# Summed weights first, a fourth staging slot, and the last feature tile held back, in a two-layer encoder trunk

## Chip, core and metric

The kernel runs on one core of a Trainium2 chip. TensorE (PE) multiplies, VectorE (DVE) and ScalarE (ACT) work element by element, GpSimd (POOL) issues some transfers and fills a few tiles, and SyncE (SP) issues most transfers. The metric is the device time of one execution in microseconds (us).

## What is computed

Two requests of 256 rows each run through the same two-layer encoder with shared weights. In front of each stand 16 meta rows, which are dropped at the end. Each layer adds a mixer (retention and grouped attention) and then a SwiGLU of width 2816 to the residual; the width of the model is 1024.

```python
def _mixer(h, w_in, ...):
    proj = h @ w_in
    rq, rk, rv, rg, aq, ak, av, gr, ga = jnp.split(proj, split_idx, axis=-1)
    ...
    merged = jax.nn.sigmoid(gr) * ret + jax.nn.sigmoid(ga) * att
    return merged @ w_out

def _swiglu(h, w_ffn_in, w_ffn_out):
    a, u = jnp.split(h @ w_ffn_in, 2, axis=-1)
    return (jax.nn.silu(a) * u) @ w_ffn_out

def _trunk(x, ...):
    h = jnp.concatenate([meta_tokens, x], axis=1)          # 16 + 256 rows
    ...
    for l in range(DEPTH):                                 # 2 layers
        h = h + _mixer(_rms(h, norm_mix[l]), w_in[l], ...)
        h = h + _swiglu(_rms(h, norm_ffn[l]), w_ffn_in[l], w_ffn_out[l])
    return _rms(h, norm_final)[:, N_META:]
```

## The kernel before

**Products.** All products keep fp32 accuracy: each operand is split into a rounded high part and the rest (`wh`, `wl` for weights, `xh`, `xl` for activations), and each tile product is three matmuls, high by high, high by low, low by high. The high part is a cast on ACT, the low part a subtraction on DVE (L214 and L215 for plain weights, L238 and L242 for the staged ones). In layer 0 a request has 272 columns, in layer 1, where the meta rows are no longer needed, 256; layer 1 takes both requests in one matmul of 512 columns where it can.

**The first matrix of the SwiGLU.** Its 22 feature tiles are done in three groups, 0 to 7, 8 to 14 and 15 to 21. The first three tiles of a layer are plain (`fa`, `fu`). The other 19 per layer are done by a seven-product scheme of the Strassen kind, `product(f, i)` for i from 0 to 6, each product four k-steps of three matmuls, twelve matmuls of 272 or 256 columns. It mixes the two requests (`T0`, `T1`, `T2` are sums of their activations) and the weights: per feature tile f there are the summed weights c (tile `wc`: the up-weights, to which two accumulating DMAs on POOL's queue, L225 and L226, add another half of the up-weights and half of the gate-weights), a (tile `wa`, the gate-weights as they are), b (tile `wb`, made on DVE from `wa` and `wc` at L250 and L251) and d (tile `wst`). Products 0 and 4 use a, 1 and 5 use b, 2 and 3 use c, 6 uses d. In the trace all of them are `sp`, or `p` for 5 and 6.

**Staging.** `wc` and `wa` of all f, and before the first f of a layer the mixed activations `xn`, share the tag `q` of three slots. A slot can be loaded again when its last reader on DVE has run: for `wc` that is the low part of c (`cl`, L242), for `wa` the low part of a (`wl`, L242). The high and low part of c have one buffer each, `ch` and `cl`.

**Order.** `plan` gives each load and each step of the splitting (`s_load`, `s_1` to `s_4`) a due time, a lead in units of four products ahead of the f that needs it. A scheduler then fixes the order of each engine's instructions; at run time every engine, and SP's and POOL's queues, go strictly in that order, so an instruction that waits holds up all behind it.

**The end of a feature tile.** After products 2 and 3, L882 to L884 combine their PSUM banks with product 1; L884 is the last reader of the bank of product 2. Products 0 to 4 take turns in a `lin` and an `att` bank. After product 6, DVE L891, tanh on ACT L892, DVE L893 and L894, a cast on ACT (`oh`, L304) and DVE L305 (`ol`) make the tile's output.

**The second matrix.** After each group, `out` runs eight output tiles j for each request (`fo`), each accumulating over all feature tiles of the group, seven or eight times three matmuls. It begins with j = 0 and 1, for both requests, and the last feature tile of the group is the last that a `fo` unit needs. In the residual `f`, L915 then adds the unit. The attention of layer 1 begins behind the last group of layer 0, with the table `rel` (L449) and the decays `dm` (L708, L709) made from it; `rope` and nine zeroed tiles (`v80`, `p80`, `pm80`) stand in a pool that is never closed.

Of the kernel before, what the change touches and what calls it, by code (L numbers as in the profile page):

```python
# [90 lines left out]
def hybrid_kernel(tc, ctx, a, y_dram):  # L91
# [13 lines left out]
    def f32(t):  # L105
        return t.bitcast(F32)
# [30 lines left out]
    def tab(i, s, c0, q=slice(None)):  # L137
        if s == BOTH:
            t = rope[q, i, M:].unsqueeze(1)
            return t.to_broadcast([t.shape[0], 2, S])  # L140
        return rope[q, i, c0:]

# [8 lines left out]
    open_tmp(0)  # L151
    cst = const.tile([P, NCST + 44], F32, name="cst")
    rope = const.tile([P, 4, N], F32, name="rope")

# [11 lines left out]
    dec = cst[:, ng + 2 * DEPTH:NCST]  # L166
    v80s = [const.tile([80, P], F32R, name=f"v80_{i}") for i in range(5)]
    p80s = [const.tile([80, N], F32R, name=f"p80_{i}") for i in range(2)]
    pm80s = [const.tile([80, 64], F32R, name=f"pm80_{i}") for i in range(2)]
    for t in v80s + p80s + pm80s:  # L170
        G.memset(f32(t), 0.0)
    turn = {"v": 0, "p": 0, "m": 0}

    def nxt(kind, ring):
        turn[kind] += 1
        return ring[(turn[kind] - 1) % len(ring)]

# [52 lines left out]

    def s_tmp(name, tag="q", bufs=3):
        return E["wk"].tile([P, KT, P], F32, tag=tag, name=name, bufs=bufs)

    def s_hi(w, nm):
        pool, tg, n, bufs = {"a": (wts, "w", KT, NW), "b": (wts, "w", KT, NW),
                             "c": (E["wk"], "c", KT, 1), "d": (E["wk"], "d", NK, 1)}[nm]
        w[nm] += [pool.tile([P, n, P], F32R, tag=tg + x, name=tg + x, bufs=bufs) for x in "hl"]
        A.copy(w[nm][1], w[nm][0])  # L238
# [6 lines left out]
    def s_1(key):  # L245
        w = wready[key[1:3]]
        s_hi(w, "a")
        va, vb, vc = w["a"][0], s_tmp("wb", "wb", 1), w["c"][0]
        w["b"] = [vb]
        V.tensor_tensor(vb[:, :NK], va[:, :NK], vc[:, NK:], ALU.add)  # L250
        V.scalar_tensor_tensor(vb[:, NK:], va[:, NK:], -1.0, vb[:, :NK], ALU.mult, ALU.subtract)  # L251

    def s_2(key):
        w = wready[key[1:3]]
        s_hi(w, "b")
        s_lo(w, "a")
# [37 lines left out]

    def mm(ps, key, hi, lo, s, c0):
# [123 lines left out]
    def L(key, s, post):  # L419
        prog.append((key, s, post))  # L420
# [4 lines left out]
    def layer(l):  # L425
# [11 lines left out]
        def open_att():  # L437
            E["nqk"], E["nqk2"], E["nv"] = NWK[l]
            if not first:
                E["c1"].close()  # L440
                open_tmp(l)
            E["xh"], E["xl"] = grid(tx + "h", F32R), grid(tx + "l", F32R)
            E["sg"] = grid("f", F32)
            E["cm"], E["c1"] = ExitStack(), ExitStack()
            mpp = E["cm"].enter_context(tc.tile_pool(name=f"mp{l}", bufs=1))
            E["mp"] = grid("mp", F32, pool=mpp)
            E["wk"] = E["c1"].enter_context(tc.tile_pool(name=f"wka{l}", bufs=1))
            E["rel"] = E["wk"].tile([P, 2, DW], F16, name="rel")
            nc.sync.dma_start(E["rel"], a["rel"])  # L449

# [51 lines left out]
        def val2(key):  # L502
            vt = st.pop(("vt", key))
            pt = att("vps")
            for c, w, i in KCH:
                T.transpose(pt[:, i * P:(i + 1) * P], vt[:, c:c + w], ident)
            v = E["wk"].tile([P, 2, 2, P], F32R, tag="v", name="v", bufs=E["nv"])
            split(v[:, 0], v[:, 1], pt[:, :2 * P].rearrange("p (c d) -> p c d", c=2))
            if first and key[2]:
                v80 = st.pop(("v80", key[:2]))  # L510
            else:
                T.transpose(pt[:M, 2 * P:3 * P], vt[:, :M], ident)
                v80 = nxt("v", v80s)
# [108 lines left out]
        def att_t(s, hq):  # L622
            ps = st.pop(("p", s, hq))
            pt = E["wk"].tile([P, 2, 2, N - q0], F32R, tag="pt", name="pt", bufs=2)
            p80 = nxt("p", p80s)
            tp = att("ptp")
# [31 lines left out]
        def meta_t(s, g):  # L658
# [6 lines left out]
            split(ptm[:, 0], ptm[:, 1], tp[:, :P].rearrange("p (c d) -> p c d", c=2))  # L665
            p80 = nxt("m", pm80s)
            A.copy(p80[0:16], tp[:M, 128:192])
# [45 lines left out]
        def ret_s(s, hr):  # L713
            q, k, dm = st.pop(("rq", s)), st.pop(("rk", s)), st["dm", hr]
            pt = E["wk"].tile([P, 2, 2, N - q0], F32R, tag="pt", name="rpt", bufs=2)
            p80 = nxt("p", p80s)
            for c, w, i in KCH:
# [97 lines left out]
        def norm_x(s, k):  # L815
            if s and k % NK == 0:
                E["xn", k // NK] = E["wk"].tile([P, NK, N - q0], F32, tag="q", name="xn", bufs=3)
            for i in (k, k + 1):
# [36 lines left out]

        def product(f, i):
            w = wready[l, f]
# [16 lines left out]
            t1, u2 = st["tu"][:, 0], st["tu"][:, 1]  # L874
            if i == 1:
                V.tensor_tensor(u2, ps, t1, ALU.subtract)
            elif i == 2:
                st["p5"] = ps
            elif i == 3:
                st["yw"], st["c"], p5 = two("yw"), two("c", 4), st.pop("p5")  # L880
                y, v = st["yw"][:, 0], st["yw"][:, 1]
                V.tensor_tensor(v, ps, u2, ALU.add)  # L882
                V.tensor_tensor(y, p5, u2, ALU.add)
                V.scalar_tensor_tensor(st["c"][:, 3], v, -1.0, p5, ALU.mult, ALU.subtract)  # L884
            elif i == 4:
                V.tensor_tensor(st["c"][:, 0], ps, t1, ALU.add)
                st["v"] = two("v")
# [48 lines left out]

        def U(kind, j, s, rhs, c0, post, *args, bank=lin):
            L((l, kind, j), s, (rhs, c0, post, args, bank))

# [125 lines left out]
        for gi, (f0, f1) in enumerate(GROUPS):  # L1065
# [44 lines left out]
    prefetch(-1)  # L1110
    nc.sync.dma_start(rope, a["rope"])
    for k in range(0, KT, 4):
        nc.sync.dma_start(E["h"][1][:, k:k + 4], a["x"][1, :, k:k + 4])
    for key, f, rest in prog:
        if key is None:
            f(*rest)
            continue
        prefetch(pos[key])
        if key[0] == "sp":
            rest[0](*rest[1:])  # L1120
            slot[0] += 0.5
        else:
            rhs, c0, post, args, bank = rest
            hi, lo = rhs()
            ps = bank(key[1])
            mm(ps, key, hi, lo, f, c0)
            slot[0] += 2 if f == BOTH else 1
            post(ps, *args)
        due(slot[0])
# [40 lines left out]
```

## Time and profile before

| | us |
|---|---|
| median of three runs | 1891.21 (1889.67 to 1892.96) |
| the profiled execution | 1892.1 |
| its span | 1890.3 |
| PE busy | 1812.6 |
| DVE busy | 1293.2 |
| ACT busy | 862.6 |

The profiled execution lies 0.9 us over the median. Times in rows are counted from the start of the span. The three groups of layer 0 run from about 590 to 930, those of layer 1 from about 1510 to 1835. A releaser in brackets is the instruction or transfer on which the idle engine waited last. The granted clock of PE is a share of 2.4 GHz; it has two levels, 2.4 and 1.2 GHz, and a window shows a mean.

### The profile page before, as it was taken

How to read it: one execution, taken by the hardware profiler on the slowest of the kernel's cores; microseconds unless marked ns; L12 is line 12 of the kernel's file. 1: busy time of each engine (PE TensorE's matmuls, PEld its weight loads, DVE VectorE, ACT ScalarE, POOL GpSimd, SP SyncE). 2: the span in 40 equal slices, each digit the busy share in tenths (PEclk: the TensorE clock that was granted, in tenths of full speed). 3: DMA queues.
4: the chain of work that ended last, by engine and by line, in shares of the span. 5: the costliest groups of instructions: out<-in, count | busy, mean ns of one | idle time of the engine just before them, and what ended most of it. 6: DMA issues, size and time to landing. Idle time of an engine off the chain costs nothing.

```text
span 1890.3 us, 33475 instructions
## 1 busy us (share of the span) xinstructions
PE 1812.6 (96%) x13002; PEld 1712.7 (91%) x13002; DVE 1293.2 (68%) x2948; ACT 862.6 (46%) x1833; POOL 76.5 (4%) x107
## 2 busy tenths in 40 slices
PE   9999999999999899799899999999999998988997
PEld 8999999999999899799898888889888987987996
DVE  7777777775468747647787677667744886575685
ACT  7777753443334424323456666434433443332443
POOL 0000000000001101001000000000000010010100
PEclk9999999999999999899999999999999999999999
DMA  4222122224225635535242221122243365364442
GB/s 149 90 71 76 60 65 68 79 79 133 90 84 134 184 84 135 138 83 147 80 133 90 68 79 57 67 90 68 69 143 101 98 158 152 93 152 124 113 126 70
DMA packets 95104, 192.73 MB, mean 102 GB/s; under 512 B 10336, under 2 KB 18784, under 8 KB 94944
## 3 DMA queue, kind: packets, MB, share of 16 engines
q1 hardware_dynamic: 81136, 163.15, 27.2%
q0 software_dynamic: 12576, 26.35, 7.6%
q8 instruction: 102, 1.67, 0.4%
q10 hardware_dynamic: 1232, 1.08, 0.2%
q14 instruction: 58, 0.48, 0.1%
HBM read 186.35 MB, written 4.19 MB: 101 GB/s over the span
## 4 chain that ended last, share of the span: by engine, by line
PE 69%; DVE 12%; DMA 11%; ACT 4%; issue 4%; DVEq 0%; POOL 0%; ACTq 0%; POOLq 0%
DMA wc<-in_w_ffn_in 6%; PE fo L299 4%; PE fo L300 4%; PE fo L301 4%; DMA wst<-in_w_ffn_out 2%; DMA wa<-in_w_ffn_in 2%; PE rv L300 2%; PE rv L299 2%; PE rv L301 2%; PE ao L300 2%; PE ao L301 2%; PE ao L299 2%; PE aq L299 2%; PE gr L301 2%; PE gr L300 2%
## 5 line engine op out<-in xcount | busy, mean ns | idle before, releaser
L214 ACT CAST wh<-wst 128x512 fp32r<-128x512 f32 (+1 forms) x424 | 250.9, 610 | 367.6 <-PE fo L300 73.9
L215 DVE TENSOR_TENSOR wl<-wst,wh 128x512 fp32r<-128x512 f32 (+1 forms) x424 | 281.7, 677 | 126.6 <-ACT wh L214 120.5
L299 PE MATMUL fo<-oh,wh 128*128 128x272 f32 (+2 forms) x616 | 190.5, 310 | 25.6 <-ACT oh L304 25.6
L300 PE MATMUL fo<-ol,wh 128*128 128x272 f32 (+2 forms) x616 | 189.9, 309 | 0.0
L301 PE MATMUL fo<-oh,wl 128*128 128x272 f32 (+2 forms) x616 | 189.2, 308 | 0.0
L299 PEld LDWEIGHTS fo<-oh,wh 128*128 128x128 f32 x616 | 119.1, 194 | 31.5 <-ACT oh L304 27.5
L300 PEld LDWEIGHTS fo<-ol,wh 128*128 128x128 f32 x616 | 119.5, 194 | 5.4 <-DVE ol L305 1.3
L301 PEld LDWEIGHTS fo<-oh,wl 128*128 128x128 f32 x616 | 119.7, 194 | 4.1
L915 DVE SCALAR_TENSOR_TENSOR f<-fo,f 128x272 f32<-128x272 f32 (+2 forms) x84 | 39.5, 471 | 110.1 <-PE fo L301 109.7
L869 PE MATMUL sp<-xh,wl 128*128 128x272 f32 (+1 forms) x304 | 87.3, 287 | 2.3 <-DVE wl L242 2.3
L867 PE MATMUL sp<-xh,wh 128*128 128x272 f32 (+1 forms) x304 | 87.4, 287 | 0.0
L868 PE MATMUL sp<-xl,wh 128*128 128x272 f32 (+1 forms) x304 | 86.9, 286 | 0.0
L238 ACT CAST wh<-wa 128x1024 fp32r<-128x1024 f32 x38 | 39.8, 1048 | 86.9 <-PE fo L300 52.4
L250 DVE TENSOR_TENSOR wb<-wa,wc 128x512 f32<-128x512 f32 x38 | 26.3, 692 | 75.3 <-DMA wc<-in_w_ffn_in 57.4
L299 PE MATMUL wo<-mh,wh 128*128 128x272 f32 (+2 forms) x224 | 67.8, 303 | 0.0
L300 PE MATMUL wo<-ml,wh 128*128 128x272 f32 (+2 forms) x224 | 67.4, 301 | 0.0
L301 PE MATMUL wo<-mh,wl 128*128 128x272 f32 (+2 forms) x224 | 67.4, 301 | 0.0
L867 PE MATMUL sp<-xh,ch 128*128 128x272 f32 (+1 forms) x152 | 46.6, 307 | 19.1 <-DVE c L884 19.0
L225 POOL DMA_DIRECT2D wc<-in_w_ffn_in x38 | 32.7, 862 | 786.4 <-DMA wc<-in_w_ffn_in 198.1
L869 PEld LDWEIGHTS sp<-xh,wl 128*128 128x128 f32 x304 | 58.0, 191 | 2.5 <-DVE wl L242 2.5
L238 ACT CAST wh<-wb 128x1024 fp32r<-128x1024 f32 x38 | 39.6, 1043 | 42.3 <-DVE wb L251 28.8
L867 PEld LDWEIGHTS sp<-xh,wh 128*128 128x128 f32 x304 | 58.2, 191 | 0.0
(428 smaller groups left out, 6412.4 us busy)
## 6 DMA issues: line engine op xcount, KB each, us to landing
wst<-in_w_in SPq DMA_DIRECT2D x208, 256.0 KB, 2.7
wc<-in_w_ffn_in SPq DMA_DIRECT2D x38, 512.0 KB, 3.6
wc<-in_w_ffn_in POOLq DMA_DIRECT2D x76, 256.0 KB, 5.8
wa<-in_w_ffn_in SPq DMA_DIRECT2D x38, 512.0 KB, 4.6
wst<-in_w_ffn_out SPq DMA_DIRECT2D x64, 256.0 KB, 3.0
wst<-in_w_ffn_in SPq DMA_DIRECT2D x62, 256.0 KB, 3.0
wst<-in_w_att_o SPq DMA_DIRECT2D x32, 256.0 KB, 2.8
wst<-in_w_ret_o SPq DMA_DIRECT2D x32, 256.0 KB, 2.8
```

The costliest lines, as they stand in the source:

```text
L214: A.copy(wh[:, k:k + n], st[:, :n])
L215: V.tensor_tensor(wl[:, k:k + n], st[:, :n], f32(wh)[:, k:k + n], ALU.subtract)
L225: nc.gpsimd.dma_start(c[:, NK:], fu[:, :NK], accum_op=ALU.add)
L238: A.copy(w[nm][1], w[nm][0])
L250: V.tensor_tensor(vb[:, :NK], va[:, :NK], vc[:, NK:], ALU.add)
L299: T.matmul(out, wh[:, k], at(hi, s, k, c0), start=(k == 0), stop=False)
L300: T.matmul(out, wh[:, k], at(lo, s, k, c0), start=False, stop=False)
L301: T.matmul(out, wl[:, k], at(hi, s, k, c0), start=False, stop=(k == kt - 1))
L867: T.matmul(ps, wh[:, o], xh[:, k], start=k == 0, stop=False)
L868: T.matmul(ps, wh[:, o], xl[:, k], start=False, stop=False)
L869: T.matmul(ps, wl[:, o], xh[:, k], start=False, stop=k == NK - 1)
L915: V.scalar_tensor_tensor(hh, of(ps, s, q0), 0.5, hh, ALU.mult, ALU.add)
```

## The change

It has three parts, and line numbers of the new kernel are 4 to 8 higher.

1. For every f but the first of a layer's 19, products run in the order 2, 3, 0, 1, 4, 5, 6: the two with the summed weights come first. The splitting goes with it: `wb` and the high part of c in `s_1`, low part of c and high of a in `s_2`, and so on, each lead a quarter larger. The combinations of L882 to L886 come after product 1, which is now the fourth.
2. The tag `q` has four slots and the pair for d two. The room comes from `rope` and the nine zeroed tiles, which move to the attention's pool and are thus loaded and zeroed once for each layer. In layer 0 SP loads `rope` behind the second request's rows; in layer 1 the nine memsets, `rope` (557 KB) and `rel` stand on POOL's queue, the memsets behind the last product of layer 0, and before the `hd` transfers (L929).
3. `out` does j = 0 and 1 in two parts: first all feature tiles but the last for every one of these units, then the last tile for every one. The fourth unit of layer 0 takes an `att` bank. This holds for `wo` too.

```diff
@@ hybrid_kernel: tables and rings
-            t = rope[q, i, M:].unsqueeze(1)
+            t = E["rope"][q, i, M:].unsqueeze(1)
...
-    cst = const.tile([P, NCST + 44], F32, name="cst")
-    rope = const.tile([P, 4, N], F32, name="rope")
+    cst = const.tile([P, NCST + 76], F32, name="cst")
...
-    v80s = [const.tile([80, P], F32R, name=f"v80_{i}") for i in range(5)]
-    p80s = [const.tile([80, N], F32R, name=f"p80_{i}") for i in range(2)]
-    pm80s = [const.tile([80, 64], F32R, name=f"pm80_{i}") for i in range(2)]
-    for t in v80s + p80s + pm80s:
-        G.memset(f32(t), 0.0)
+    def open_rings():
+        wk = E["wk"]
+        E["rope"] = wk.tile([P, 4, N], F32, name="rope")
+        E["v"] = [wk.tile([80, P], F32R, name=f"v80_{i}") for i in range(5)]
+        E["p"] = [wk.tile([80, N], F32R, name=f"p80_{i}") for i in range(2)]
+        E["m"] = [wk.tile([80, 64], F32R, name=f"pm80_{i}") for i in range(2)]
+        for t in E["v"] + E["p"] + E["m"]:
+            G.memset(f32(t), 0.0)
@@ staging slots and split steps
-    def s_tmp(name, tag="q", bufs=3):
+    def s_tmp(name, tag="q", bufs=4):
...
-                             "c": (E["wk"], "c", KT, 1), "d": (E["wk"], "d", NK, 1)}[nm]
+                             "c": (E["wk"], "c", KT, 1), "d": (E["wk"], "d", NK, 2)}[nm]
...
-        s_hi(w, "a")
         va, vb, vc = w["a"][0], s_tmp("wb", "wb", 1), w["c"][0]
         w["b"] = [vb]
         V.tensor_tensor(vb[:, :NK], va[:, :NK], vc[:, NK:], ALU.add)
         V.scalar_tensor_tensor(vb[:, NK:], va[:, NK:], -1.0, vb[:, :NK], ALU.mult, ALU.subtract)
+        s_hi(w, "c")
 
     def s_2(key):
         w = wready[key[1:3]]
-        s_hi(w, "b")
-        s_lo(w, "a")
+        s_lo(w, "c")
+        s_hi(w, "a")
 
     def s_3(key):
         w = wready[key[1:3]]
-        s_hi(w, "c")
-        s_lo(w, "b")
+        s_lo(w, "a")
+        s_hi(w, "b")
 
     def s_4(key):
         w = wready[key[1:3]]
+        s_lo(w, "b")
         s_hi(w, "d")
-        s_lo(w, "c")
         s_lo(w, "d")
...
-                    lead = (2.5, 1, 0.75, 0.5, 0.25) if last[0] == "sp" else (3, 2, 2, 1, 1)
+                    lead = (2.75, 1.25, 1, 0.75, 0.5) if last[0] == "sp" else (3, 2, 2, 1, 1)
@@ mm: a unit in two parts
-        for k in range(kt):
+        for k in range(kt)[slice(None) if part is None else slice(-1) if part == 0 else slice(-1, None)]:
@@ opening of the attention's pool
-            nc.sync.dma_start(E["rel"], a["rel"])
+            open_rings()
+            for t, src in ((E["rope"], a["rope"]), (E["rel"], a["rel"])):
+                (nc.sync if first else nc.gpsimd).dma_start(t, src)
@@ product
+            if i in (2, 3):
+                st["p", i] = ps
             if i == 1:
-                V.tensor_tensor(u2, ps, t1, ALU.subtract)
-            elif i == 2:
-                st["p5"] = ps
-            elif i == 3:
-                st["yw"], st["c"], p5 = two("yw"), two("c", 4), st.pop("p5")
+                V.tensor_tensor(st["tu"][:, 1], ps, st["tu"][:, 0], ALU.subtract)
+            if i == (1 if wait else 3):
+                st["yw"], st["c"], p5, u2 = two("yw"), two("c", 4), st["p", 2], st["tu"][:, 1]
                 y, v = st["yw"][:, 0], st["yw"][:, 1]
-                V.tensor_tensor(v, ps, u2, ALU.add)
+                V.tensor_tensor(v, st["p", 3], u2, ALU.add)
@@ out, and the loop over feature tiles
-                for s in ss:
-                    for j in js:
-                        U(kind, j, s, rhs, q0, post, s, j, *args)
+                for part in (0, 1) if js[0] == 0 else (None,):
+                    for s in ss:
+                        for j in js:
+                            bank = att if (s, j) == (1, 1) and part == 0 else lin
+                            U(kind, j, s, rhs, q0, post, s, j, *args, bank=bank, part=part)
...
-                for i in range(7):
-                    L(("sp", l, f, i), None, (product, f, i))
+                wait = f > n
+                for n_, i in enumerate((2, 3, 0, 1, 4, 5, 6) if wait else range(7)):
+                    L(("sp", l, f, n_), None, (product, f, i, wait))
@@ main
-    nc.sync.dma_start(rope, a["rope"])
```

On SP, in group 1 of layer 0, the loads of the staged weights. Before:

```order
L228 DMA wst_9604<-in_w_ffn_in 128x512
L224 DMA wc_9602<-in_w_ffn_in 128x1024
L227 DMA wa_9603<-in_w_ffn_in 128x1024
L228 DMA wst_9738<-in_w_ffn_in 128x512
L224 DMA wc_9736<-in_w_ffn_in 128x1024
L227 DMA wa_9737<-in_w_ffn_in 128x1024
L228 DMA wst_9872<-in_w_ffn_in 128x512
```

After:

```order
L232 DMA wst_9719<-in_w_ffn_in 128x512
L231 DMA wa_9584<-in_w_ffn_in 128x1024
L228 DMA wc_9717<-in_w_ffn_in 128x1024
L232 DMA wst_9853<-in_w_ffn_in 128x512
L231 DMA wa_9718<-in_w_ffn_in 128x1024
L228 DMA wc_9851<-in_w_ffn_in 128x1024
L217 DMA wst_10044<-in_w_ffn_out 128x512
```

Before, the feature tiles follow as `wc_9468`, `wc_9602`, `wc_9736`; after, as `wc_9449`, `wc_9583`, `wc_9717`. Before, `wc_9736` takes the slot of `wc_9468`, so it waits for `cl_9627`, and `wa_9737` that of `wa_9603`. After, `wc_9717` takes the slot of `wa_9450`, two tiles back, and waits for the low part of that; `wa_9718` takes the slot of `wc_9449` and waits for `cl_9562`.

On DVE at the same place, one feature tile. Before (`sp_9580` and `sp_9561` are products 3 and 2, `p34` holds 5 and 6):

```order
L250 TENSOR_TENSOR wb_9711<-wa_9603,wc_9602 128x512
L883 TENSOR_TENSOR yw_9593<-sp_9561,tu_9545 128x272
L305 TENSOR_TENSOR ol_9255<-v_9490,oh_9254 128x2x272
L251 SCALAR_TENSOR_TENSOR wb_9711<-wa_9603,wb_9711 128x512
L882 TENSOR_TENSOR yw_9593<-sp_9580,tu_9545 128x272
L242 TENSOR_TENSOR cl_9627<-wc_9468,ch_9626 128x1024
L884 SCALAR_TENSOR_TENSOR c_9594<-yw_9593,sp_9561 128x272
L886 TENSOR_TENSOR c_9594<-sp_9610,tu_9545 128x272
L242 TENSOR_TENSOR wl_9709<-wa_9603,wh_9708 128x1024
```

After:

```order
L253 TENSOR_TENSOR wb_9692<-wa_9584,wc_9583 128x512
L902 TENSOR_TENSOR v_9494<-v_9494,c_9472 128x544
L254 SCALAR_TENSOR_TENSOR wb_9692<-wa_9584,wb_9692 128x512
L246 TENSOR_TENSOR cl_9562<-wc_9449,ch_9561 128x1024
L310 TENSOR_TENSOR ol_9263<-v_9494,oh_9262 128x2x272
L885 TENSOR_TENSOR tu_9577<-sp_9591,tu_9577 128x272
L889 TENSOR_TENSOR yw_9605<-sp_9545,tu_9577 128x272
L890 TENSOR_TENSOR yw_9605<-sp_9532,tu_9577 128x272
L891 SCALAR_TENSOR_TENSOR c_9606<-yw_9605,sp_9532 128x272
L894 TENSOR_TENSOR c_9606<-sp_9614,tu_9577 128x272
L246 TENSOR_TENSOR wl_9715<-wa_9584,wh_9714 128x1024
```

In both, `yw` and `c` (L882 to L886, after L889 to L894) belong to a tile, `cl` to the next one and `wb` to the one behind that. Now all of `wb` and `cl` stands ahead of these combinations; before, `cl` stood between them and the first half of `wb` ahead of them. `cl_9562` now serves the first product of its tile; `cl_9627` served the third.

On PE, the first `fo` units behind group 1 of layer 0. Before (j = 0 is `fo1_10197`, j = 1 is `fo1_10230`, both of the first request), where the last feature tile of the group is reached after 28 matmuls:

```order
L301 MATMUL fo1_10230<-oh_9254,wl_10113 128x272
L299 MATMUL fo1_10230<-oh_9254,wh_10112 128x272
L299 MATMUL fo1_10197<-oh_9254,wh_10042 128x272
L300 MATMUL fo1_10230<-ol_9255,wh_10112 128x272
L301 MATMUL fo1_10230<-oh_9254,wl_10113 128x272
L299 MATMUL fo1_10230<-oh_9254,wh_10112 128x272
L300 MATMUL fo1_10230<-ol_9255,wh_10112 128x272
L301 MATMUL fo1_10230<-oh_9254,wl_10113 128x272
```

After, at the end of the first part:

```order
L304 MATMUL fo1_10264<-oh_9262,wh_10111 128x272
L305 MATMUL fo1_10264<-ol_9263,wh_10111 128x272
L306 MATMUL fo1_10264<-oh_9262,wl_10112 128x272
L304 MATMUL fo1_10197<-oh_9262,wh_10042 128x272
L305 MATMUL fo1_10197<-ol_9263,wh_10042 128x272
L306 MATMUL fo1_10197<-oh_9262,wl_10043 128x272
L304 MATMUL fo1_10226<-oh_9262,wh_10111 128x272
L305 MATMUL fo1_10226<-ol_9263,wh_10111 128x272
```

Before, 28 matmuls of two units stand ahead of the first one with the last feature tile; now there are 72, of four units, and the twelve with the last tile follow.

On DVE at the end of layer 0. Before:

```order
L894 TENSOR_TENSOR v_11542<-v_11542,c_11524 128x544
L708 TENSOR_SCALAR dm_14501<-rel_12143,lg_115 128x416
L709 SCALAR_TENSOR_TENSOR dm_14501<-rel_12143,lg_115,dm_14501 128x416
L305 TENSOR_TENSOR ol_10643<-v_11542,oh_10642 128x2x272
L915 SCALAR_TENSOR_TENSOR f_6080<-fo2_11587,f_6080 128x272
```

After:

```order
L902 TENSOR_TENSOR v_11542<-v_11542,c_11524 128x544
L310 TENSOR_TENSOR ol_10651<-v_11542,oh_10650 128x2x272
L715 TENSOR_SCALAR dm_14521<-rel_12143,lg_96 128x416
L716 SCALAR_TENSOR_TENSOR dm_14521<-rel_12143,lg_96,dm_14521 128x416
L923 SCALAR_TENSOR_TENSOR f_6080<-fo2_11587,f_6080 128x272
```

`ol`, the last piece of the last feature tile, now stands ahead of the two `dm` rows, and the `fo` sums still stand behind them.

## Rows read from the trace of the kernel before

**Rows 1.** The page, part 1: busy time, share of the span and instructions of each engine.

```profile
PE 1812.6 (96%) x13002; PEld 1712.7 (91%) x13002; DVE 1293.2 (68%) x2948; ACT 862.6 (46%) x1833; POOL 76.5 (4%) x107
```

**Rows 2.** Waits of PE: waiter, waited for, us in total, times, longest.

```profile
PE fo L299 <- ACT oh L304: 25.6, 5, 7.0
PE sp L867 <- DVE c L884: 19.0, 11, 3.5
PE sp L869 <- DVE cl L242: 6.3, 10, 0.9
PE sp L869 <- DVE wl L242: 5.1, 4, 2.3
```

**Rows 3.** Waits of DVE, the same columns: the staged summed weights.

```profile
DVE wb L250 <- DMA wc<-in_w_ffn_in: 57.4, 19, 4.0
```

**Rows 4.** Windows: length, busy of PE, PEld, DVE, ACT, POOL, granted PE clock, DMA share, GB/s.

```profile
590.00:648.00 58.00, 55.92 (x441) 55.31 (x440) 47.59 (x76) 26.78 (x42) 10.46 (x12) 1.00 0.69 178
648.00:734.00 86.00, 81.30 (x635) 81.08 (x634) 46.77 (x75) 26.65 (x40) 5.24 (x6) 0.98 0.44 116
734.00:787.00 53.00, 47.27 (x342) 46.09 (x342) 40.54 (x66) 20.40 (x34) 7.01 (x8) 0.94 0.57 134
787.00:804.00 17.00, 10.00 (x58) 9.78 (x58) 7.75 (x13) 2.83 (x6) 0.00 (x0) 0.70 0.43 127
830.00:1000.00 170.00, 161.23 (x1256) 159.99 (x1255) 127.17 (x254) 77.52 (x147) 10.55 (x12) 0.98 0.43 116
1510.00:1650.00 140.00, 130.61 (x930) 122.50 (x929) 92.06 (x144) 50.08 (x77) 13.96 (x16) 0.96 0.52 138
1650.00:1710.00 60.00, 52.94 (x408) 51.41 (x407) 46.75 (x77) 25.17 (x42) 8.73 (x10) 0.94 0.59 144
1710.00:1835.00 125.00, 112.60 (x812) 106.58 (x811) 80.12 (x131) 43.27 (x71) 8.76 (x10) 0.93 0.45 117
```

**Rows 5.** Line 224 from 736 to 781: issues, ns each, first and last start.

```profile
L224 SPq DMA_DIRECT2D wc<-in_w_ffn_in x4: 327/328/328, 738.1 to 779.1; - x4
```

**Rows 6.** The same line from 1650 to 1706.

```profile
L224 SPq DMA_DIRECT2D wc<-in_w_ffn_in x5: 328/328/328, 1652.0 to 1703.3; - x5
```

**Rows 7.** Timeline, 738 to 752: start, us, engine, line, operation [idle before, releaser].

```profile
738.06 0.33 SPq L224 DMA_DIRECT2D wc<-in_w_ffn_in  x1
...
747.23 0.69 DVE L250 TENSOR_TENSOR wb<-wa,wc 128x512 f32<-128x512 f32 x1 [2.78 <-DMA wc<-in_w_ffn_in]
...
750.24 1.22 DVE L242 TENSOR_TENSOR cl<-wc,ch 128x1024 fp32r<-128x1024 f32 x1
...
751.51 0.39 PE L869 MATMUL sp<-xh,cl 128*128 128x272 f32 x1 [0.56 <-DVE cl L242]
```

**Rows 8.** Timeline, 786 to 798: the end of group 1 in layer 0.

```profile
786.56 0.29 PE L299 MATMUL fo<-oh,wh 128*128 128x272 f32 x1
...
791.77 0.51 ACT L214 CAST wh<-wst 128x384 fp32r<-128x384 f32 x1 [5.35 <-DMA wst<-in_w_ffn_out]
...
793.76 0.72 DVE L891 TENSOR_TENSOR c<-p,yw 128x544 f32<-128x544 f32 x1
...
796.54 0.65 ACT L304 CAST oh<-v 128x544 fp32r<-128x544 f32 x1 [1.20 <-DVE v L894]
...
797.24 0.59 PE L299 MATMUL fo<-oh,wh 128*128 128x272 f32 x1 [7.00 <-ACT oh L304]
```

**Rows 9.** Timeline of PE, 1720 to 1722: the end of group 1 in layer 1.

```profile
1720.94 0.79 PE L299 MATMUL fo<-oh,wh 128*128 128x512 f32 x1 [6.38 <-ACT oh L304]
```

**Rows 10.** The page, part 6: issues, KB each, median us to landing.

```profile
wa<-in_w_ffn_in SPq DMA_DIRECT2D x38, 512.0 KB, 4.6
```

**Rows 11.** Timeline of DVE, 919 to 934: the end of layer 0.

```profile
927.19 0.44 DVE L708 TENSOR_SCALAR dm<-rel,lg 128x416 f32<-128x416 f16 x1 [0.18 <-DMA rel<-in_rel]
```

**Rows 12.** Line 171, the rings' first memsets: ns min/median/max, first and last start.

```profile
L171 POOL MEMSET v<- x5: 194/194/201, 0.9 to 1.8; 80x128 f32 x5
```

**Rows 13.** Line 929, two DMAs on POOL's queue: from issue to landing.

```profile
DMA to landing us min/median/max: 5.3/5.7/6.2
```

More of the change, by code (lines that the diff above doesn't have):

```diff
@@ L138, in tab @@
         if s == BOTH:
-            t = rope[q, i, M:].unsqueeze(1)
+            t = E["rope"][q, i, M:].unsqueeze(1)
             return t.to_broadcast([t.shape[0], 2, S])
-        return rope[q, i, c0:]
+        return E["rope"][q, i, c0:]
     E = {"h": grid("f", F32)}
@@ L166, in hybrid_kernel, with nxt @@
     dec = cst[:, ng + 2 * DEPTH:NCST]
-    v80s = [const.tile([80, P], F32R, name=f"v80_{i}") for i in range(5)]
-    p80s = [const.tile([80, N], F32R, name=f"p80_{i}") for i in range(2)]
-    pm80s = [const.tile([80, 64], F32R, name=f"pm80_{i}") for i in range(2)]
-    for t in v80s + p80s + pm80s:
-        G.memset(f32(t), 0.0)
-    turn = {"v": 0, "p": 0, "m": 0}
-    def nxt(kind, ring):
+    turn = {"v": 0, "p": 0, "m": 0}
+    def open_rings():
[6 more added lines that the diff above has]
+            G.memset(f32(t), 0.0)
+    def nxt(kind):
         turn[kind] += 1
-        return ring[(turn[kind] - 1) % len(ring)]
+        return E[kind][(turn[kind] - 1) % len(E[kind])]
     lg = const.tile([P, DEPTH * 8], F32, name="lg")
@@ L293, in prefetch, with mm @@
             fn(key)
-    def mm(ps, key, hi, lo, s, c0):
+    def mm(ps, key, hi, lo, s, c0, part=None):
         wh, wl, kt = wready[key]
         out = of(ps, s, c0)
-        for k in range(kt):
+        for k in range(kt)[slice(None) if part is None else slice(-1) if part == 0 else slice(-1, None)]:
             T.matmul(out, wh[:, k], at(hi, s, k, c0), start=(k == 0), stop=False)
@@ L512, in val2 @@
                 T.transpose(pt[:M, 2 * P:3 * P], vt[:, :M], ident)
-                v80 = nxt("v", v80s)
+                v80 = nxt("v")
                 mp = pt[:M, 2 * P:3 * P]
@@ L624, in att_t @@
             pt = E["wk"].tile([P, 2, 2, N - q0], F32R, tag="pt", name="pt", bufs=2)
-            p80 = nxt("p", p80s)
+            p80 = nxt("p")
             tp = att("ptp")
@@ L665, in meta_t @@
             split(ptm[:, 0], ptm[:, 1], tp[:, :P].rearrange("p (c d) -> p c d", c=2))
-            p80 = nxt("m", pm80s)
+            p80 = nxt("m")
             A.copy(p80[0:16], tp[:M, 128:192])
@@ L715, in ret_s @@
             pt = E["wk"].tile([P, 2, 2, N - q0], F32R, tag="pt", name="rpt", bufs=2)
-            p80 = nxt("p", p80s)
+            p80 = nxt("p")
             for c, w, i in KCH:
@@ L816, in norm_x @@
             if s and k % NK == 0:
-                E["xn", k // NK] = E["wk"].tile([P, NK, N - q0], F32, tag="q", name="xn", bufs=3)
+                E["xn", k // NK] = E["wk"].tile([P, NK, N - q0], F32, tag="q", name="xn", bufs=4)
             for i in (k, k + 1):
@@ L852, in two, with product @@
             return E["tmp"].tile([P, n, N - q0], F32, tag="t4", name=name, bufs=1)
-        def product(f, i):
+        def product(f, i, wait):
             w = wready[l, f]
@@ L873, in product @@
                 return
-            t1, u2 = st["tu"][:, 0], st["tu"][:, 1]
+            if i in (2, 3):
+                st["p", i] = ps
             if i == 1:
-                V.tensor_tensor(u2, ps, t1, ALU.subtract)
-            elif i == 2:
-                st["p5"] = ps
-            elif i == 3:
-                st["yw"], st["c"], p5 = two("yw"), two("c", 4), st.pop("p5")
+                V.tensor_tensor(st["tu"][:, 1], ps, st["tu"][:, 0], ALU.subtract)
+            if i == (1 if wait else 3):
+                st["yw"], st["c"], p5, u2 = two("yw"), two("c", 4), st["p", 2], st["tu"][:, 1]
                 y, v = st["yw"][:, 0], st["yw"][:, 1]
-                V.tensor_tensor(v, ps, u2, ALU.add)
+                V.tensor_tensor(v, st["p", 3], u2, ALU.add)
                 V.tensor_tensor(y, p5, u2, ALU.add)
@@ L885, in product @@
             elif i == 4:
+                t1 = st["tu"][:, 0]
                 V.tensor_tensor(st["c"][:, 0], ps, t1, ALU.add)
@@ L935, in layer, with U @@
         MM = lambda: (E["mh"], E["ml"])
-        def U(kind, j, s, rhs, c0, post, *args, bank=lin):
-            L((l, kind, j), s, (rhs, c0, post, args, bank))
+        def U(kind, j, s, rhs, c0, post, *args, bank=lin, part=None):
+            L((l, kind, j), s, (rhs, c0, post, args, bank, part))
         pair = (0, 1) if first else (BOTH,)
@@ L1101, in hybrid_kernel @@
     plan()
+    held = {}
     ps = att("warm")
@@ L1122, in hybrid_kernel @@
         else:
-            rhs, c0, post, args, bank = rest
+            rhs, c0, post, args, bank, part = rest
             hi, lo = rhs()
-            ps = bank(key[1])
-            mm(ps, key, hi, lo, f, c0)
+            ps = held.pop((key, f)) if part == 1 else bank(key[1])
+            mm(ps, key, hi, lo, f, c0, part)
+            if part == 0:
+                held[key, f] = ps
+                continue
             slot[0] += 2 if f == BOTH else 1
```

## The prediction

> **What bounds the kernel now.** I read the page first, then the waits of PE, the windows, and the timeline around two of the waits. PE is busy 96% of the span [rows 1], so a change that takes no matmul away can only win idle time and time at the lower clock. The waits show where idle time of that kind stands. Behind the feature-tile groups PE waits 25.6 us in five places for `oh`, the last tile's output, and inside the groups 19.0, 6.3 and 5.1 us for three pieces of DVE's work [rows 2]: 56.0 us, all of it in the stretches 648 to 1000 and 1510 to 1835.
>
> The windows add the clock. Over 590 to 648 it is full and PE busy 55.9 of 58 us; over 787 to 804, where PE is idle for 7.0 us, the mean is 0.70, between the two levels of 2.4 and 1.2 GHz [rows 4]. Each window's length times what its clock lacks of one gives 1.7 + 3.2 + 5.1 + 3.4 + 5.6 + 3.6 + 8.8 = 31.4 us. A part of that is counted twice, because PE was idle while the clock was low; in 787 to 804, 7.0 of 17 us were idle, which is 2.1 of the 5.1, and I take 2 more for the rest (an estimate). 27 us remain. So 56 + 27 = **83 us** are what the three parts of the change can reach.
>
> Next, why PE waits inside the groups. One matmul takes 55.92/441 = 0.127 us [rows 4], a tile of 84 thus 10.7 us in layer 0, and 10.0 with 256 columns in layer 1. But `wc` is issued every (779.1 - 738.1)/3 = 13.7 us [rows 5], and every (1703.3 - 1652.0)/4 = 12.8 us in layer 1 [rows 6]. The timeline shows the ring that sets this. `wc` is issued at 738.06; 9.2 us later, at 747.23, `wb` begins, DVE having waited 2.78 us for that weight; at 750.24 `cl` begins, and it ends at 751.46; PE, which had waited for it, goes on at 751.51 [rows 7]. The next `wc` needs a slot that `cl` frees: 9.2 us of transfers and 4.2 us of DVE, once for every tile, 13.4 us. DVE's 57.4 us of waiting for `wc` [rows 3] are the same thing over 19 tiles. While DVE waits there, the combinations that free the PSUM bank of product 2 wait behind `wb`, and PE for them.
>
> And why it waits behind the groups. In layer 0, group 1, the last product ends at 786.56. ACT stands until 791.77 before a cast of a `fo` weight that was late; L891 comes at 793.76, the `oh` cast at 796.54, PE at 797.24 after 7.00 us of idleness [rows 8]. PE had only 28 matmuls to do in the meantime.
>
> **The change, part by part.** No product and no weight byte is added but one more load of the tables.
>
> *The fourth slot.* `wc` of a tile now takes the slot of an `wa` two tiles back. The ring from the low part of one `wa` to that of the second next one is 9.2 us of transfers and less than DVE's whole work for a tile. That work is bounded by the windows: 40.54 us of 53 in 734 to 787 [rows 4], by 53/13.7 tiles, is 10.5 us, and 46.75 us in 60/12.8 tiles is 10.0 in layer 1. So at most 19.7 us for two tiles, 9.9 each, and 9.6 in layer 1: under PE's 10.7 and 10.0. The other ring, from `cl` to the load of `wa` in that slot, to `wb` and to the next `cl`, is 4.6 us [rows 10] and four pieces on DVE, of which `wb` takes 0.69 and `cl` 1.22 [rows 7]; with the same again for the other two it is 8.4 us for each tile. Both fit. By the tiles' sizes the transfers are 1.84 MB for each tile, which is then 172 GB/s, or 183 in layer 1; 590 to 648 shows 178 GB/s with PE at 55.9 of 58 us [rows 4].
>
> *Summed weights first, splitting a quarter earlier.* `cl` is now made for the next tile while its predecessor's first two products run, and the bank that L884 frees is asked for a whole tile later. That takes the 19.0, 6.3 and 5.1 us their ground, as long as the rings close. The steps are the same instructions. What is new is that ACT's cast into `ch`, and `cl` behind it, must wait for PE's second product, 24 x 0.127 = 3.0 us into the tile, with the rest of DVE's row queued behind `cl`; `cl` is done at about 5.4 us (3.0, then 1.22 for `cl` and, an estimate, as much for the cast of the same tile) and wanted at 10.7. I cost it at nothing, because 5 us cover it. Without that cover it is the slower rival below.
>
> What of the stalls inside the groups stays: the first of a layer's 19 tiles keeps the old order, and DVE's 10.0 us for each tile of layer 1 leave nothing beside PE's 10.0, though some of it are splits of `fo` weights that spill over a group's end. The bounds are 0 and half of what is there; with the clock shared out by idle time that is 30.4 + 27 x 30.4/56 = 45, half 22.5. I take **10 us**, nearer to 0, because both rings close.
>
> *`out` in two parts.* Now 72 matmuls stand ahead of the last tile in groups 1 and 2 of layer 0, 9.1 us instead of 3.6; 84 in group 0. In layer 1 they are 36 (42) of 512 columns instead of half as many; at two times 0.119 us that is 4.3 (5.0) us more. The cover grows by 5.5 (6.4) and 4.3 (5.0) us. The longest wait, 7.00 us [rows 8], leaves 1.5 us; the 6.38 us of group 1 in layer 1 [rows 9] leave 2.1; the other three are 12.2 us together and should go, but for 0.3. That is 3.9, with the lower clock behind such a wait (830 to 1000, with a wait in it, lacks 3.4 us [rows 4]) about **7 us**. Bounds: 0, if the chain starts earlier for a faster group, and 23, in the second rival.
>
> *Tables.* In layer 0 the rings of zeros are made at the start as before, and `rope` changes places on SP with the second request's rows, on which more work hangs; I take nothing. At the end of layer 0 nine memsets of about 0.2 us [rows 12] wait for the last product, then `rope` and `rel` are issued on POOL; landing takes 5.3 to 6.2 us for the transfers there [rows 13], so that `rel` is there some 8 to 10 us behind the last product. `dm`, which waited 0.18 us [rows 11], stands before the `fo` sums, and the first of these is due when the parts of 9.1 and 0.4 us are over. What waits behind it is DVE's sum, which holds a PSUM bank, and thus PE. Bounds 0 and, with a landing 3 us later, 3; I take **1 us**. The two `hd` transfers stand behind on POOL, and wait for `fo` sums that end later.
>
> The sum: 83 - 10 - 7 - 1 = 65 us. 1892.1 - 65 = 1827.1 us for an execution like the profiled one, which lies 0.9 over the median: **1826 us**.
>
> The clock's 27 us are worth one more look. After idle stretches the windows show the lower level, and 31.4 us in all. The Trainium skill (TensorE: Matmul & The Clock Gate, Part 1) holds that the ramp costs under 1% of a typical kernel's span, which would be at most 18.9 us here, an estimate from that page. By it the reach would be 75 us and the time 1834. The rows show more than that, and I go by the rows.
>
> **Rivals.**
>
> *The staging or DVE still sets the pace.* At 178 GB/s the mean busy share of the DMA engines is 0.69, against 0.57 in 734 to 787 [rows 4]; if they take longer for it, or DVE in layer 1 is the bound, half of the 45 us stays, 12.5 more than I took: 1839 us. Against it: 590 to 648 runs at that rate.
>
> *The last tile is late as before.* ACT goes in order, and the 5.35 us before 791.77 were for a `fo` weight [rows 8]. If with denser transfers such weights come later still, tanh and `oh` are late by as much as the new cover: 23 of the 38 us (25.6 and its share of the clock) stay instead of 7, which gives 1842 us. Both together: 1855.
>
> *Slower.* `ch` has one buffer, and now it is written while its reader is the tile's beginning. If little of DVE's row runs beside the first two products and the cast (4.1 us), a tile takes up to 4.1 + 10.5 = 14.6 us, 3.9 more than PE's 10.7, and as much more in layer 1: 38 x 3.9 = 148 us on 1892.1 - 83, or 1956 by the median. It costs more than all is worth from 83/38 = 2.2 us for each tile on, 12.9 us in layer 0, that is with less than 1.7 us of DVE's work hidden there. Against it: in DVE's order `wb` and the last tile's L901 and L902 stand ahead of `cl`, and none of them needs `ch`.
>
> *No change.* SP goes in order. If a `wst` load that waits for a later `dl` stands ahead of the loads that have a slot, the fourth slot is empty while it waits and the period stays at 13.4 us, with the `fo` waits taken over by the next late weight: 1891.
>
> **How the numbers follow.** The forecast 0.59; staging or DVE 0.17 (1839); late last tile 0.12 (1842); both 0.05 (1855); no change 0.03; slower 0.04. The range begins at 1804, where nothing of the 83 us stays and the 4 us taken off as counted twice are real, and goes to 1848, past the first two rivals with some room for 3 us at the border; about 0.84 of the chance lies there with the ends of the forecast's own spread taken off. About 0.2%, 3.8 us, can be told from no change. Faster 0.93, same 0.03, slower 0.04.
>
> **What would show it.** Right: `wc` is issued every 10 to 11 us; DVE's wait for `wc` falls from 57.4 to under 15; PE's waits on L884's successor and on `cl` are nearly gone; waits on `oh` are at most 2 us each; the granted clock is 0.98 or more over both stretches. Wrong: a period over 12 us; DVE's waits moved to `wa`, or to ACT's `ch`; a wait of more than 3 us for `rel`; or PE's excess moved to the weights of `fo`.

## The result and the profile after

The changed kernel takes 1804.2 us (1803.2 to 1804.8, four runs) against 1890.4 (1883.3 to 1893.0, four runs): 0.9549 of the time before, 95% interval 0.9522 to 0.9576. The spans of the two profiled executions are 1890.3 and 1801.4 us, 88.9 apart. The forecast was 1826 with a range from 1804 to 1848, so the time lies at the very foot of the range: the mechanism is there, and I left 22 us too much standing. Two of the four runs lie below 1804; the section on the prediction says what part of the hit is luck.

The page of the changed kernel, part 1, answers to [rows 1]:

```profile
PE 1781.6 (99%) x13002; PEld 1690.1 (94%) x13002; DVE 1295.1 (72%) x2948; ACT 869.6 (48%) x1833; POOL 79.0 (4%) x118
```

The same number of matmuls, and 31.0 us less busy time: a matmul at the lower clock counts as longer (0.43 us against 0.29 for 272 columns, shown below). The waits of PE, longest first, answer to [rows 2]:

```profile
PE css L343 <- DVE p L644: 1.4, 2, 0.8
PE fa L304 <- ACT xh L309: 1.2, 4, 0.4
PE warm L1119 <- DVE lnscb L161: 1.1, 1, 1.1
PE sp L875 <- ACT wh L242: 0.9, 2, 0.7
```

All that [rows 2] shows is gone: no wait of the SwiGLU on `oh`, none on the combinations, none on `cl` or another low part of a staged weight. The last line is two waits of 0.2 and 0.7 us for a cast of a staged weight; waits of that kind took 0.8 us before. Line 253 is the first half of `wb`; what DVE still waited for ahead of it stands for the 57.4 us of [rows 3]:

```profile
L253 DVE TENSOR_TENSOR wb<-wa,wc x38: 683/688/694, 592.7 to 1723.9; 128x512 f32<-128x512 f32 x38
...
  DMA wa<-in_w_ffn_in: 0.4, 2
```

Windows with the columns of [rows 4]. By the count of matmuls the first two hold nearly the work of 590 to 648 and 648 to 1000 there; the third holds most of 1510 to 1835 and some 43 us of work behind it:

```profile
590.00:648.00 58.00, 57.82 (x459) 57.60 (x459) 53.89 (x87) 30.05 (x47) 10.48 (x12) 1.00 0.77 204
648.00:960.00 312.00, 312.00 (x2486) 311.57 (x2485) 226.87 (x415) 132.66 (x232) 23.55 (x35) 1.00 0.47 127
1480.00:1790.00 310.00, 309.26 (x2363) 297.32 (x2363) 234.79 (x391) 135.82 (x217) 29.73 (x34) 1.00 0.53 139
```

PE is busy through both stretches, and the granted clock, 0.70 to 0.98 there before, is 1.00. In the first window the transfers run at 204 GB/s, more than in any window of [rows 4], and PE waits 0.2 us.

SP's timeline in group 1 of layer 0 shows the period that [rows 5] had at 13.7 us:

```profile
702.77 0.33 SPq L228 DMA_DIRECT2D wc<-in_w_ffn_in  x1
705.54 0.33 SPq L232 DMA_DIRECT2D wst<-in_w_ffn_in  x1
709.15 0.33 SPq L231 DMA_DIRECT2D wa<-in_w_ffn_in  x1
713.30 0.33 SPq L228 DMA_DIRECT2D wc<-in_w_ffn_in  x1
```

713.30 less 702.77 is 10.5 us, PE's own tile. PE sets the pace now, and the transfers follow.

The end of the same group, ACT's timeline, answers to [rows 8]. PE's first `fo` matmul there, the end of the products, is at 766.80:

```profile
767.63 0.51 ACT L218 CAST wh<-wst 128x384 fp32r<-128x384 f32 x1 [1.65 <-DMA wst<-in_w_ffn_out]
768.05 0.43 ACT L900 ACTIVATE v<-c 128x272 f32<-128x272 f32 x1
770.22 0.65 ACT L309 CAST oh<-v 128x544 fp32r<-128x544 f32 x1 [1.74 <-DVE v L902]
```

ACT still stands before a late weight, but for 1.65 us instead of 5.35, and `oh` is ready at 770.87, 4.1 us behind the products instead of 10.6. With 9.1 us of matmuls in between, 5 us are to spare.

The end of layer 0 on DVE answers to [rows 11]:

```profile
890.01 0.44 DVE L715 TENSOR_SCALAR dm<-rel,lg 128x416 f32<-128x416 f16 x1 [2.15 <-DMA rel<-in_rel]
890.49 0.65 DVE L716 SCALAR_TENSOR_TENSOR dm<-rel,lg,dm 128x416 f32<-128x416 f16 x1
892.76 1.20 DVE L923 SCALAR_TENSOR_TENSOR f<-fo,f 128x272 f32<-128x272 f32 x3 [1.62 <-PE fo L306]
```

`rel` on POOL's queue is late for DVE by 2.15 us, but DVE then waits another 1.62 for PE, so nothing on PE hangs on the late table.

### The profile page after: what moved, and what is told of

Read it like the earlier page. It is cut to its first block, busy times and chain, and to the rows that moved or that the text cites. A ratio compares the mean times of both kernels' runs of the same rounds, so it can differ in the third digit from the quotient of the medians.

```text
span 1801.4 us, 33453 instructions
## 1 busy us (share of the span) xinstructions
PE 1781.6 (99%) x13002; PEld 1690.1 (94%) x13002; DVE 1295.1 (72%) x2948; ACT 869.6 (48%) x1833; POOL 79.0 (4%) x118
## 4 chain that ended last, share of the span: by engine, by line
PE 89%; DVE 5%; ACT 3%; issue 1%; DMA 1%; SPq 0%; DVEq 0%; ACTq 0%
PE sp L875 5%; PE sp L877 5%; PE sp L876 5%; PE fo L304 5%; PE fo L306 5%; PE fo L305 5%; PE p L877 2%; PE p L876 2%; PE p L875 2%; PE rv L304 2%; PE rv L305 2%; PE rv L306 2%; PE ao L304 2%; PE ao L305 2%; PE ao L306 2%; PE aq L304 2%
## 5 line engine op out<-in xcount | busy, mean ns | idle before, releaser
L304 PE MATMUL fo<-oh,wh 128*128 128x272 f32 (+2 forms) x616 | 185.9, 302 | 0.0
L306 PE MATMUL fo<-oh,wl 128*128 128x272 f32 (+2 forms) x616 | 185.5, 301 | 0.0
L305 PE MATMUL fo<-ol,wh 128*128 128x272 f32 (+2 forms) x616 | 185.5, 301 | 0.0
L305 PEld LDWEIGHTS fo<-ol,wh 128*128 128x128 f32 x616 | 115.8, 188 | 4.0
L242 ACT CAST ch<-wc 128x1024 fp32r<-128x1024 f32 x38 | 40.0, 1052 | 39.7 <-PE sp L876 32.9
L876 PEld LDWEIGHTS sp<-xl,wh 128*128 128x128 f32 x304 | 57.2, 188 | 0.0
L246 DVE TENSOR_TENSOR wl<-wb,wh 128x1024 fp32r<-128x1024 f32 x38 | 46.5, 1224 | 10.7 <-ACT wh L242 10.7
```

Of the source, the lines that this page charges most:

```text
L246: V.tensor_tensor(t, v, f32(h), ALU.subtract)
L876: T.matmul(ps, wh[:, o], xl[:, k], start=False, stop=False)
```

## Experiments

Two theories were to be told apart. One, of the prediction: the ring of slots sets the pace inside the groups, the two-part outputs take away the waits behind them, and each is worth what its waits show. The other: the order of products and the earlier splitting do the work, or one part makes the next one superfluous. Every ratio is against the kernel before on the same chip.

### The outputs in two parts alone

The kernel before with part 3 of the change.

```diff
...
-                for s in ss:
-                    for j in js:
-                        U(kind, j, s, rhs, q0, post, s, j, *args)
+                for part in (0, 1) if js[0] == 0 else (None,):
+                    for s in ss:
+                        for j in js:
+                            bank = att if (s, j) == (1, 1) and part == 0 else lin
+                            U(kind, j, s, rhs, q0, post, s, j, *args, bank=bank, part=part)
...
```

> The kernel before with the two-part outputs alone; order of products, three slots and tables as before. The theory of the prediction: the chain of the last tile stays as late as before, the cover grows by 4.3 to 6.4 us, so the waits on oh fall from 25.6 to about 4 us and the whole is some 31 us faster, 1860, while the 30.4 us of waits inside the groups stay. Rival, that the last tile is late because the whole group is: the same here, since the group stays slow; it differs in the next run. Rival that the gain comes from the groups alone: under 10 us, 1880 or more.

1865.5 us, 0.9867 (0.9841 to 0.9892): 26.6 us under the 1892.1 of the kernel before beside it, where 31 were expected. Its waits of PE:

```profile
PE sp L867 <- DVE c L884: 23.4, 12, 3.5
PE sp L869 <- DVE cl L242: 5.9, 9, 0.9
PE sp L869 <- DVE wl L242: 4.3, 5, 1.7
PE fo L299 <- ACT oh L304: 3.3, 3, 1.5
```

Of 25.6 us behind the groups 3.3 are left, the longest 1.5. The prediction's sum had 3.9 left, of which 1.5 in group 1 of layer 0 and 2.1 in group 1 of layer 1. The waits inside the groups are 33.6 here instead of 30.4, which may be why some of the gain is missing.

### The change without the two parts

```diff
-                for part in (0, 1) if js[0] == 0 else (None,):
+                for part in (None,):
```

> The changed kernel with its outputs in one part as before. Theory of the prediction: the waits on oh come back, 25 us and their clock, 1804 + 38 = 1842. Rival: with the group running freely oh is ready some 4.0 us behind the last product (887.1 against 883.1 at the end of layer 0 in the changed kernel), just past the 3.6 us of 28 matmuls, so that each of the six ends costs a few tenths to 2 us: 1806 to 1814.

1809.9 us, 0.9568 (0.9546 to 0.9590), 5.7 over the changed kernel. PE's waits for `oh`:

```profile
PE fo L304 <- ACT oh L309: 3.2, 2, 2.2
```

Two waits, 3.2 us. The rival has it: what the two-part outputs were for is mostly gone once the groups run freely, because `oh` then comes 4 us behind the products. The two gains overlap: 26.6 us for part 3 by itself, 5.7 on top of the rest. The 5.7 are small: the two ratios, 0.9568 and 0.9549, have intervals that overlap, though none of the four times here (1806.7 to 1810.5) reaches down to the changed kernel's.

### Three slots

```diff
-    def s_tmp(name, tag="q", bufs=4):
+    def s_tmp(name, tag="q", bufs=3):
...
-                E["xn", k // NK] = E["wk"].tile([P, NK, N - q0], F32, tag="q", name="xn", bufs=4)
+                E["xn", k // NK] = E["wk"].tile([P, NK, N - q0], F32, tag="q", name="xn", bufs=3)
```

> The changed kernel with three slots again; new order, new leads, tables moved, outputs in two parts. Theory of the prediction, the ring of slots sets the pace: wc is issued every 13 us again and some 45 us come back, 1850. Rival, the order and the earlier splitting are what counts: at most 10 us come back, 1814.

1843.8 us, 0.9752 (0.9723 to 0.9781): 39.6 us over the changed kernel. The waits of PE, and under them the wait of DVE for the staged weight:

```profile
PE sp L875 <- ACT tu L880: 22.5, 15, 2.9
PE sp L877 <- DVE cl L246: 4.5, 10, 1.6
PE sp L875 <- ACT ch L242: 3.2, 2, 1.7
```

```profile
DVE wb L253 <- DMA wc<-in_w_ffn_in: 47.8, 19, 3.3
DVE wb L253 <- DMA wa<-in_w_ffn_in: 20.6, 8, 5.4
```

DVE waits for `wc` again, 19 times as in [rows 3]; only the names that PE waits for have changed with the order.

### Four slots with the old order

The changed kernel with `wait = False`, the old steps of splitting and the old leads.

```diff
...
-                    lead = (2.75, 1.25, 1, 0.75, 0.5) if last[0] == "sp" else (3, 2, 2, 1, 1)
+                    lead = (2.5, 1, 0.75, 0.5, 0.25) if last[0] == "sp" else (3, 2, 2, 1, 1)
...
-                wait = f > n
+                wait = False
```

> The changed kernel with the old order of products, the old steps of splitting and the old leads; four slots, tables moved, outputs in two parts. Theory of the prediction: the fourth slot closes the ring, so most stays, 1804 to 1815. Rival, the order counts: the combinations of a tile and cl still stand behind the wait for wb on DVE, and 20 to 45 us come back, 1825 to 1850.

1803.0 us, 0.9535 (0.9511 to 0.9560), as fast as the changed kernel within the intervals. DVE no longer waits for `wc` here either; what it waits for ahead of `wb` is this:

```profile
DVE wb L254 <- DMA wa<-in_w_ffn_in: 5.5, 10, 0.8
```

So the order of products with its splitting and leads, the first thing that the change names, is worth nothing that shows beside the fourth slot and the two parts.

### New order, old leads

The lead line alone goes back, as above.

> The changed kernel with the old leads (2.5, 1, 0.75, 0.5, 0.25) and all else as changed. If the transfers' ring is all that counts: 1803 to 1806. If a quarter more lead is needed because the first product of a tile now wants cl: cl comes a product or two late for each tile, 10 to 40 us lost, 1814 to 1845.

1804.4 us, 0.9544 (0.9512 to 0.9577). The quarter more of lead is worth nothing that shows either.

### The slot alone

Old order, old leads, outputs in one part: the edits of "Four slots with the old order" and "The change without the two parts" together. The moved tables and the second pair for d stay.

> Old order, old leads, outputs in one part; only the four slots and the second pair for d, with the tables moved. Theory after the first runs, the slot is what counts and the two-part outputs are worth 6 us once the groups run freely: 1806 to 1814. Rival, order or parts must be there with the slot: 1825 or more.

1814.4 us, 0.9595 (0.9553 to 0.9637), at the upper end of what was expected. The slot alone brings 76 to 78 of the 86 to 89 us (69 to 85 by the interval of its ratio). The second pair for d came along; with three slots it brings nothing that shows (next run), and four slots without it were not run. PE's waits for `oh` in it:

```profile
PE fo L304 <- ACT oh L309: 6.9, 4, 2.9
```

With the two parts added ("Four slots with the old order", 1803.0) these 6.9 us go, and 11.4 us of time with them. Without the two parts the new order waits 3.2 us for `oh` and the old one 6.9, and the times are 1809.9 and 1814.4; the intervals of the two ratios overlap, so whether the order is worth a little there stays open.

### Three slots with the old order

The run with the two parts alone, plus the tables moved and the second pair for d.

```diff
...
-                             "c": (E["wk"], "c", KT, 1), "d": (E["wk"], "d", NK, 1)}[nm]
+                             "c": (E["wk"], "c", KT, 1), "d": (E["wk"], "d", NK, 2)}[nm]
...
-            nc.sync.dma_start(E["rel"], a["rel"])
+            open_rings()
+            for t, src in ((E["rope"], a["rope"]), (E["rel"], a["rel"])):
+                (nc.sync if first else nc.gpsimd).dma_start(t, src)
...
```

> Three slots, old order and leads, outputs in two parts, and the tables moved with the second pair for d: the run with the parts alone (1865.5) plus the move. If the move and the pair are worth nothing: 1862 to 1869, and then the reordering alone is worth about 22 us at three slots (against the 1843.8 of the changed kernel with three slots). If the move of the tables costs at the end of layer 0, as the 1 to 3 us of the prediction: 1867 to 1870. If the pair for d is what the three-slot run lived on: 1850 or less.

1867.2 us, 0.9870 (0.9853 to 0.9888), against 0.9867 for the parts alone: the move of the tables and the pair cost and bring nothing that shows. And it gives the order, with its splitting and leads, a price without the slot: 1867.2 to 1843.8, 23 us. DVE's wait for `wc`, 47.8 us with the new order and three slots, is longer here:

```profile
DVE wb L254 <- DMA wc<-in_w_ffn_in: 72.4, 19, 4.9
```

### How much the rings have to spare

The first load of one staged weight, `wa` or `wc`, is issued twice into its slot; once with the changed kernel, once with the old order and leads.

```diff
-        nc.sync.dma_start(v, fa)
+        for _ in range(2):
+            nc.sync.dma_start(v, fa)
```

> The changed kernel with each wa loaded twice into its slot. Ring of one tile from cl to wa, wb and the next cl: in the changed kernel 6.1 us of landing and 3.1 us of DVE, 9.2 of 10.6; the second load adds some 3 us, so the ring is 12 us, 1.6 over PE's tile, and most of 38 tiles lose it: 1804 + 40 to 60. Rival, the order has slack that takes it up: under 15 us lost.

> The same double load of wa with the old order and leads and four slots. If the ring alone counts: the same loss as with the new order, 40 to 60 us. If the order is what buys slack: at least 15 us more lost here than with the new order.

> The changed kernel with the first load of each wc doubled. This ring spans two tiles: 8.1 us from issue to the first accumulation's landing and 7.3 us of DVE, 15.4 of 21.1, so 3 us more change nothing by it; wa stands behind it in the queue and may land 1 to 2 us later. Under 10 us lost. Rival, the bandwidth is the limit: the same loss as with wa doubled.

> The same double load of wc with the old order and leads and four slots. Ring alone: under 10 us lost, as with the new order. Order buys slack: 15 us or more lost here.

`wa` twice: 1847.9 us with the new order (0.9769, 0.9706 to 0.9833), 1819.2 with the old (0.9618, 0.9586 to 0.9650). `wc` twice: 1830.8 and 1834.2 (0.9679, 0.9627 to 0.9730; 0.9697, 0.9666 to 0.9728). Each is the median of two runs; those of `wa` in the new order lie 9 us apart, 1843.5 and 1852.3. Two of the four expectations missed: `wa` with the old order lost 16 us, neither as much as with the new nor more, and `wc` with the new order lost 27 instead of under 10 (31 with the old order, so the order buys little slack there). The second load costs more than the 3 us I gave it, as SP's timeline shows for `wa` in the new order, and then in the old:

```profile
704.60 7.26 SPq L232 DMA_DIRECT2D wa<-in_w_ffn_in  x2
711.97 0.37 SPq L228 DMA_DIRECT2D wc<-in_w_ffn_in  x1
```

```profile
702.03 0.33 SPq L232 DMA_DIRECT2D wa<-in_w_ffn_in  x1
703.59 0.33 SPq L228 DMA_DIRECT2D wc<-in_w_ffn_in  x1
706.08 0.33 SPq L232 DMA_DIRECT2D wa<-in_w_ffn_in  x1
```

The second load of a slot waits for the first to land, about 7 us in the one and 4 in the other, and in the new order the `wc` behind it on SP waits too. Summed over the kernel, SP waits 184 us for a first landing of `wa` in the new order and 109 in the old. So these runs do not weigh the rings cleanly, the two orders did not get the same delay, and the 512 KB more for each tile are not told apart from the wait. They do show two things. The kernel has less to spare than a second landing with its traffic, whichever weight it is. And the same edit costs the new order more than the old (44 us lost against 16), where I had expected the same or the reverse. The trace suggests a reason beside the longer delay: in the changed kernel `wa` goes out at 709.15, behind `wc` at 702.77 and so beside its accumulations, while with the old order `wa` goes first; from issue to landing it takes 5.8 us against 4.8 in the median over 650 to 960. That this is the whole reason was not tried.

## Where the prediction was right and where it was wrong

*What bounds the kernel.* Right. The four kinds of wait in [rows 2] are the ones that went, and nothing took their place: what PE still waits for, 1.4 us at most of a kind, it waited for before.

*The number.* The range reached 1804.2 by 0.2 us, and that is luck in part. Its foot was drawn where nothing of the 83 us stays, which came true, and where the 4 us taken off as counted twice are real after all, which did not; losses that I had not counted stood in for them, as the next paragraph shows.

*The reach, 83 us.* Too small: 88.9 us went by the spans. The two pages split it. PE's idle time (span less busy) fell from 77.7 to 19.8 us, by 57.9, and its busy time by 31.0. [rows 2] had named 56.0 of the idle time. The busy time is not all the clock's, because each wait is listed short. PE's timeline before, at the wait of [rows 8], shows how, and behind the wait it shows the lower clock:

```profile
789.96 0.29 PE L299 MATMUL fo<-oh,wh 128*128 128x272 f32 x1
797.24 0.59 PE L299 MATMUL fo<-oh,wh 128*128 128x272 f32 x1 [7.00 <-ACT oh L304]
797.64 0.43 PE L300 MATMUL fo<-ol,wh 128*128 128x272 f32 x1
```

The matmul at 789.96 shows 0.29 us, and the next would have started 0.127 later, so 7.28 - 0.127 = 7.15 us were lost where the idle time says 7.00. Over the 30 waits of [rows 2] that is some 5 us (an estimate), which the page counts as busy; some 26 of the 31.0 are left for the clock. So the 27 us of the prediction held, and taking 4 us off the 31.4 as counted twice was right in size. What the sum lacked are these 5 us and 1.9 us in smaller waits: 56.0 + 1.9 + 5 + 26 = 88.9.

*The fourth slot.* Right, and shown: three slots in the changed kernel cost 39.6 us, and four slots in the old order, with the two parts, bring all. The sum for the ring, at most 9.9 us for a tile, fits: `wc` is issued every 10.5 us, which is PE's own tile, and PE never waited for it.

*Summed weights first.* Here the prediction gave the order the ground of the 30.4 us "as long as the rings close". The runs part the two: with four slots and the two parts the order brings nothing that shows, with three it brings 23 us. The prediction did not say which of the two edits carried the gain; had it priced them one by one, the old order with four slots would have come out equal by its own ring sum.

*What stays inside the groups, 10 us.* Wrong; of the waits named 0 stayed. DVE's 10.0 us for a tile of layer 1, which I held against PE's 10.0, included splits of `fo` weights, and over the whole stretch DVE is busy 234.8 of 310 us. The first of the 19 tiles, in its old order, waits 0.2 us in layer 0 and 0.7 in layer 1, for a cast.

*What stays behind the groups, 7 us.* Wrong for the changed kernel, right for the parts alone. I held the chain of the last tile at 10.6 us, as before. Alone, the two parts left 3.3 us where 3.9 were forecast. In the changed kernel the chain takes 4.1 us, since the weight that ACT stood before comes sooner; the waits on `oh` were in good part made by the stalls inside the group: the slot alone takes them from 25.6 to 6.9 us. I had named a chain that starts earlier as the lower bound, and chose the other.

*Tables, 1 us.* 0: `rel` came 6.9 us behind the products (889.99 against 883.12), less than the 8 to 10 that I worked out, and the run with the tables moved shows no price.

*The clock.* By the rule of the Trainium skill (TensorE: Matmul & The Clock Gate, Part 1), under 1% of the span, I had worked out 1834 us; the trace does not agree: the mean clock went from 0.982 to 0.998, and by the split above some 26 us came back with it, over the 18.9 that the rule would allow. The prediction went by the rows, and rightly.

*Rivals.* Neither of the two in between came: 590 to 648 now runs at 204 GB/s with 0.2 us of waiting on PE. The slower one, the single `ch`, did not come: `cl` runs from 707.90 to 709.12 and the tile that needs it begins at 713.93. No stall on it shows with four slots; with three, PE waited 3.2 us for `ch`.

## What to carry to other kernels

Write the ring of each staging slot out as a loop (last reader, issue, landing, the engine's work up to the next last reader) and divide by the tiles it spans: one more slot made it span two, and that, with the second pair for d, was worth 76 of 86 us without the other parts. Price parts of a change alone and on top of each other: waits behind a stalled stage are partly that stage's own stalls, handed on, and a cover bought for them is worth little once it runs freely (26.6 us alone, 5.7 on top). A microsecond of PE's idle time in many short waits cost more than itself here: 56.0 us of listed waits stood for 88.9.

## What the runs showed of the hardware

The factor between listed waits and time is of a kind in three places: 56.0 us listed for 88.9 in the whole change, 6.9 for 11.4 (slot alone against slot with parts) and 3.2 for 5.7 (the change without parts): 1.6 to 1.8. The last two rest on small differences between runs that were not made side by side. In the whole change the clock is the larger share of the excess, some 26 of 32.9 us; in the last of these it was 0.99 over 648 to 960, against 1.00 in the changed kernel. With transfers at 204 GB/s, a mean busy share of 0.77 of the DMA engines, PE waited 0.2 us in 590 to 648.
